# A top-k bisection step with two VectorE operations instead of three

## The chip, the cores and the metric

The kernel runs on one core of a Trainium2 chip. TensorE (PE in the profile, its weight loads PEld) multiplies matrices, VectorE (DVE) and ScalarE (ACT) work elementwise, GpSimd (POOL) does next to nothing here, and SyncE (SP) issues the DMA transfers. The metric is the device time of one execution in microseconds (us), lower being better.

## The reference

The reference is one layer of a decoder: a feed-forward half-step, a mixer of three attention branches, and a second feed-forward half-step, on 1024 rows of width 1024. What matters here is the second branch, in which each query attends to its 256 best keys. An indexer scores all earlier keys of a query; the 256th largest score of each row is the threshold.

```python
# dsa_attention, per block of 128 queries
sc = jnp.einsum('bqhd,bkd->bqhk', iqi, ik)
score = jnp.einsum('bqh,bqhk->bqk', iwi, jax.nn.relu(sc))
score = jnp.where(key_pos <= qpos, score, -jnp.inf)
_, idx = lax.top_k(score, 256)      # the selected keys
...
s = jnp.einsum('bqhd,bqkd->bqhk', qi, gather(k, idx)) * scale
p = jax.nn.softmax(jnp.where(valid, s, -jnp.inf), axis=-1)
```

The other two branches are a forgetting attention (8 heads of 64, called fox heads below) and an attention to 256 memory tokens (4 heads of 128, memory heads).

## The kernel before

Rows are handled in 8 blocks of 128. Matrices are multiplied in fp32 as high and low parts, so an operand is made by a ScalarE cast (`wH`, `th`, `ph`) and a VectorE subtraction (`wL`, `tl`, `pl`). The program runs in stages: first feed-forward half, the combined projection, the attention heads, the merge of the branches, second feed-forward half.

**The selection.** The first two blocks of rows have at most 256 keys, so only blocks 2 to 7 are selected. `select` (L937) finds the threshold of each of 128 rows by bisection over the bits of a 32-bit float. One pass is an ACTIVATE with Sign on ScalarE: it adds the candidate `nf` (tile `sn`, one number per row) to the scores `wk` (128 rows by 384 to 1024 columns), throws the result away (`junk`) and leaves the sum of the signs in `cnt` (`scnt`). From the sum VectorE makes the next candidate: `k` (`sk`) is the bit or 0, `m` (`sm`) collects the accepted bits, and `nf` is `m` with the next bit tried, flipped by `fm` (`sf`). There are 31 such steps after a first pass that finds the sign: 32 passes a block, 192 in all. A tail of about ten VectorE operations follows (`sy`, `sq`, a scan over `wk`, `mk`), which makes the mask.

**What the selection runs beside.** It is the background of two stages. In the projection stage the column blocks are mq, iq, fk, fq, fv and dq. Each chain step multiplies 24 matmuls into a bank `tm`, squares the bank on ScalarE (`hsq`), takes a sum and a reciprocal root on VectorE (`hv`, `rs_y`, `rs_a`), scales, transposes on TensorE (`turn`), and splits (`th`, `tl`). The dq blocks also rotate (`rot`), four more VectorE operations. In the attention stage first the four memory heads run, then the eight fox heads, then the eight selected heads. A head's row block is a chain: scores on TensorE (`spm` in a memory head, `sp` in the others), a row maximum on VectorE (`nmx`), the exponential on ScalarE (`ns`), transposes on TensorE (`pT`), the split `ph`, `pl`, and a product with the values (`po`). The projection of the gates (`gate`, 24 matmuls for half a tile, ended by `sg`) is filler: independent TensorE work that is put between the chains.

**What sets the order.** All engines work through their queues in order. The order is written at build time by a planner, `_Flow` (L77): it keeps a clock per engine, charges each recorded operation a cost, and lets the chain go on whose time has come. A VectorE operation on one column is charged 0.06 + 0.00105 us, after a wait of 0.13 us behind an operation of the same engine or 0.2 us behind another (L81, L91 to L96):

```python
LAT, SAME = 0.2, 0.13
wait = self.LAT if self.last != eng else 0.0 if eng == "PE" else self.SAME
start = max(self.clk[eng], self.t + wait)
```

The selection is the `background` of both runs (L1544, L1617): it is stepped whenever its time is not past the TensorE clock of the plan. `finish` (L1556) writes out whatever is left. The tile framework then places the recorded instructions in each engine's queue by its own reckoning of readiness, so the final order is read from the built program. In it, instructions that the helper classes record all have line 51.

Of the kernel before, what the change touches and what calls it, by code (L numbers as in the profile page):

```python
# [12 lines left out]
I32 = mybir.dt.int32  # L13
AF = mybir.ActivationFunctionType
OP = mybir.AluOpType
# [4 lines left out]
P = 128  # L20
# [135 lines left out]
def trunk_layer_kernel(  # L156
# [7 lines left out]
    T, A, V = fl.T, fl.A, fl.V  # L164
# [7 lines left out]
    def load(o, i):  # L172
        nc.sync.dma_start(plain(o), plain(i))

    def store(o, i):
        nc.sync.dma_start(plain(o), plain(i))
# [760 lines left out]
    def select(sp, t):  # L937
        n = (t + 1) * P
        wk = sp.tile([P, S], F32, tag="work", name="wk", bufs=3)[:, :n]
        load(wk, sc_s[t][:, :n])  # L940
        fl.t += 4.0
        yield
        junk = sp.tile([P, S], BF16, tag="junk", name="junk", bufs=1)[:, :n]
        m, k, fm, nf = [sp.tile([P, 1], I32, tag=nm, name=nm, bufs=3) for nm in ("sm", "sk", "sf", "sn")]
        cnt = sp.tile([P, 1], F32, tag="scnt", name="scnt", bufs=3)
        V.memset(m, 0)
        thr = 511.0 - n
        A.activation(junk, wk, AF.Sign, accum_out=cnt)
        V.tensor_scalar(k, cnt, thr, -1.0, op0=OP.is_ge, op1=OP.mult)
        V.tensor_scalar(fm, k, 0x7FFFFFFF, None, op0=OP.bitwise_xor)  # L950
        for b in range(30, -1, -1):
            V.scalar_tensor_tensor(nf, m, 1 << b, fm, op0=OP.bitwise_or, op1=OP.bitwise_xor)
            yield
            A.activation(junk, wk, AF.Sign, bias=nf.bitcast(F32)[:, 0:1], accum_out=cnt)
            V.tensor_scalar(k, cnt, thr, float(1 << b), op0=OP.is_ge, op1=OP.mult)
            V.tensor_tensor(m, m, k, op=OP.bitwise_or)
        V.tensor_tensor(nf, m, fm, op=OP.bitwise_xor)
        V.tensor_scalar(nf, nf, -2147483648, None, op0=OP.bitwise_xor)
        lo = nf.bitcast(F32)

        y = sp.tile([P, S], BF16, tag="sy", name="sy", bufs=1)[:, :n]
        q = sp.tile([P, S], BF16, tag="sq", name="sq", bufs=1)[:, :n]
        c2 = sp.tile([P, 4], F32, tag="sc2", name="sc2", bufs=2)
        V.tensor_scalar(y, wk, lo[:, 0:1], 0.0, op0=OP.is_gt, op1=OP.add, accum_out=c2[:, 0:1])
        yield
        V.tensor_scalar(y, wk, lo[:, 0:1], 3e38, op0=OP.is_le, op1=OP.mult)
        V.tensor_tensor_reduce(out=q, in0=y, in1=wk, scale=1.0, scalar=3e38, op0=OP.add, op1=OP.min,
                               accum_out=c2[:, 1:2])
        yield
        V.tensor_scalar(c2[:, 0:1], c2[:, 0:1], 255.5, None, op0=OP.is_gt)  # L970
        V.copy_predicated(lo, c2[:, 0:1].bitcast(I32), c2[:, 1:2])
        V.tensor_scalar(y, wk, lo[:, 0:1], 0.0, op0=OP.is_gt, op1=OP.add, accum_out=c2[:, 2:3])
        V.tensor_scalar(c2[:, 3:4], c2[:, 2:3], -1.0, 256.0, op0=OP.mult, op1=OP.add)
        yield
        V.tensor_scalar(q, wk, lo[:, 0:1], None, op0=OP.is_equal)
        yield
        one = sp.tile([P, 1], F32, tag="one", name="one", bufs=1)
        V.memset(one, 1.0)
        V.tensor_tensor_scan(wk, one.to_broadcast([P, n]), q, 0.0, OP.mult, OP.add)
        yield  # L980
        V.scalar_tensor_tensor(q, wk, c2[:, 3:4], q, op0=OP.is_le, op1=OP.mult)
        V.tensor_tensor(y, y, q, op=OP.add)
        mk = sp.tile([P, S], BF16, tag="mk", name="mk", bufs=1)[:, :n]
        V.tensor_scalar(mk, y, 1.0, BIG, op0=OP.subtract, op1=OP.mult)
        store(mask_s[t][:, :n], mk)
        yield
# [389 lines left out]
    cs, sn = tp.tile([P, NT, 32], F32, name="rope_cos"), tp.tile([P, NT, 32], F32, name="rope_sin")  # L1376
# [117 lines left out]
    def selection():  # L1494
        active, nxt = [], 2
        while active or nxt < NT:
            while len(active) < 2 and nxt < NT and nxt in sel_ready:
                active.append(chain(select(sel, nxt), start=fl.clk["PE"]))
                nxt += 1
            if not active:  # L1500
                yield fl.clk["PE"] + 5.0
                continue
            c = min(active, key=lambda c: c.t)
            fl._step(c)
            active = [c for c in active if not c.done]
            yield min([c.t for c in active], default=fl.clk["PE"])
# [111 lines left out]
    op = right["op"]  # L1618
# [97 lines left out]
```

## Time and profile before

| | |
|---|---|
| Time, median of 3 runs | 2552.32 us (2551.23 to 2557.42) |
| The profiled execution's own time | 2555.42 us |
| Its span, first to last instruction | 2553.4 us |
| Busy: TensorE / VectorE / ScalarE | 2426.6 / 1641.0 / 1146.6 us |
| First and last Sign pass of the selection | starts at 888.6 and 1368.7 us |
| Mean granted TensorE clock | 0.978 of full speed |

The profile is one execution taken by the hardware profiler. A row of its timeline gives the start in us from the beginning of the span, the duration, engine, line, operation and tiles (out<-in), and in brackets how long the engine was idle before and what ended the wait. TensorE's instructions overlap, so their pace is read from the starts.

### The profile page before, as it was taken

The page shows a single profiled execution, that of the slowest core. Times are in us where ns is not written, and L with a number is a line of the kernel's source. Part 1 is how long each engine was busy: PE and PEld are TensorE (multiplying, and loading weights), DVE is VectorE, ACT ScalarE, POOL GpSimd, SP SyncE. Part 2 cuts the span into 40 slices and gives each one's busy share as a digit, 9 for nine tenths or more (in the row PEclk, how much of TensorE's full clock was granted, in tenths as well). Part 3 has the DMA queues.
Part 4 walks back from the last instruction along what each step waited for, and adds up shares of the span by engine and source line. Part 5 has one row for each costly group of instructions (what it writes and reads, how often), then busy time and mean ns, then how long its engine had stood idle before and what let it go on. Part 6 is the DMA issues. An engine that isn't in the chain of part 4 may idle for free.

```text
span 2553.4 us, 31738 instructions
## 1 busy us (share of the span) xinstructions
PE 2426.6 (95%) x11532; PEld 2007.0 (79%) x11532; DVE 1641.0 (64%) x3405; ACT 1146.6 (45%) x1904; POOL 2.2 (0%) x40
## 2 busy tenths in 40 slices
PE   6999999999999999989999998999979999999998
PEld 4788888888777878767777886877768888888887
DVE  7855555488757578685667556777376554554885
ACT  5533333333433366657886555543144333333332
POOL 0000000000000000000000000000000000000000
PEclk9899999999999999998999999999989999999999
DMA  7222222474334534544455535756422222225743
GB/s 232 75 80 78 91 84 79 158 302 137 127 123 144 158 106 133 157 141 147 122 156 141 146 108 177 235 173 226 169 85 66 91 66 91 91 71 191 271 151 129
DMA packets 297900, 351.64 MB, mean 138 GB/s; under 512 B 18792, under 2 KB 199688, under 8 KB 297744
## 3 DMA queue, kind: packets, MB, share of 16 engines
q1 hardware_dynamic: 297744, 349.62, 42.8%
q8 instruction: 90, 1.47, 0.2%
q14 instruction: 66, 0.54, 0.1%
HBM read 254.98 MB, written 93.54 MB: 136 GB/s over the span
## 4 chain that ended last, share of the span: by engine, by line
PE 72%; DVE 12%; ACT 7%; DMA 5%; issue 4%; SPq 0%; ACTq 0%; DVEq 0%
PE gx L51 19%; PE gy L51 14%; PE tm L51 8%; PE dx L51 8%; PE dy L51 7%; PE gate L51 6%; ACT junk L51 3%; PE br L51 3%; DVE wL L51 2%; PE po L51 2%; PE pT L51 2%; PE sp L51 2%; DMA wS<-in_w_in 1%; DMA bg<-g_s 1%; ACT ns L51 1%
## 5 line engine op out<-in xcount | busy, mean ns | idle before, releaser
L51 ACT CAST wH<-wS 128x1024 fp32r<-128x1024 f32 x238 | 225.5, 953 | 303.1 <-PE gy L51 102.8
L51 PE MATMUL gx<-th,wH 128*128 128x512 f32 x880 | 318.3, 394 | 7.2 <-ACT th L51 7.2
L51 DVE TENSOR_TENSOR wL<-wS,wH 128x1024 fp32r<-128x1024 f32 x238 | 260.3, 1099 | 88.4 <-ACT wH L51 87.7
L51 PE MATMUL gx<-th,wL 128*128 128x512 f32 x704 | 275.5, 391 | 0.0
L51 PE MATMUL tm<-wH,uh 128*128 128x512 f32 x496 | 200.5, 405 | 9.2 <-ACT wH L51 5.6
L51 PE MATMUL gy<-th,wH 128*128 128x512 f32 x528 | 206.3, 391 | 1.2 <-ACT th L51 1.2
L51 PE MATMUL gx<-tl,wH 128*128 128x512 f32 x528 | 205.4, 389 | 0.0
L51 PE MATMUL gy<-th,wL 128*128 128x512 f32 x528 | 205.4, 389 | 0.0
L51 PE MATMUL gy<-tl,wH 128*128 128x512 f32 x528 | 205.4, 389 | 0.0
L51 ACT ACTIVATE junk<-wk,sn 128x384 bf16<-128x384 f32 (+5 forms) x186 | 164.3, 883 | 89.4 <-DVE sn L51 77.2
L51 PEld LDWEIGHTS gx<-th,wH 128*128 128x128 f32 x880 | 167.5, 191 | 43.1 <-ACT th L51 8.0
L51 PE MATMUL tm<-wL,uh 128*128 128x512 f32 x496 | 197.0, 397 | 1.8 <-DVE wL L51 1.0
L51 PE MATMUL tm<-wH,ul 128*128 128x512 f32 x496 | 196.6, 396 | 0.0
L51 ACT CAST wH<-S 128x1024 fp32r<-128x1024 f32 x88 | 92.3, 1051 | 170.3 <-PE gy L51 167.0
L51 DVE TENSOR_TENSOR wL<-S,wH 128x1024 fp32r<-128x1024 f32 x88 | 107.5, 1223 | 87.8 <-ACT wH L51 87.8
L51 DVE TENSOR_TENSOR gu<-gu,gy 128x512 f32<-128x512 f32 x88 | 60.3, 685 | 157.3 <-PE gy L51 81.6
L51 PE MATMUL gate<-uh,wH 128*128 128x512 f32 x384 | 157.5, 410 | 0.0
L51 DVE TENSOR_TENSOR pl<-pT,ph 128x512 fp32r<-128x512 f32 (+1 forms) x176 | 109.8, 637 | 73.6 <-ACT ph L51 72.9
L51 PEld LDWEIGHTS gx<-th,wL 128*128 128x128 f32 x704 | 133.3, 189 | 27.8
L51 PE MATMUL gate<-uh,wL 128*128 128x512 f32 x384 | 153.4, 400 | 0.0
L51 PE MATMUL gate<-ul,wH 128*128 128x512 f32 x384 | 153.0, 398 | 0.0
L51 PE MATMUL dx<-wH 128*128 128x512 f32 x352 | 137.5, 391 | 2.2 <-DVE rows L51 2.1
(265 smaller groups left out, 5196.9 us busy)
## 6 DMA issues: line engine op xcount, KB each, us to landing
wS<-in_ffn_w_down SPq DMA_DIRECT2D x70, 512.0 KB
wS<-in_w_in SPq DMA_DIRECT2D x48, 512.0 KB
wS<-in_ffn_w_gate SPq DMA_DIRECT2D x44, 512.0 KB
wS<-in_ffn_w_up SPq DMA_DIRECT2D x44, 512.0 KB
hid_s<-gu SPq DMA_DIRECT2D x44, 512.0 KB
a<-hid_s SPq DMA_DIRECT2D x30, 512.0 KB
g_s<-sg SPq DMA_DIRECT2D x48, 256.0 KB
bg<-g_s SPq DMA_DIRECT2D x48, 256.0 KB
```

Source lines behind the costliest of these rows:

```text
L51: return fn(*a, **k)
```

## The change

The tiles `m` and `fm` are dropped. `nf` itself is carried from step to step: it starts as the first candidate; after a pass `k` is the bit if it is *not* accepted (`is_lt` instead of `is_ge`), and one operation flips that bit back and the next bit over. After the last bit the sign bit is flipped in the same way, so the two operations behind the loop go too, and the memset ahead of it. A step has two VectorE operations instead of three, `select` 64 instead of 98; over six blocks that is 204 fewer. The Sign passes and the tail are as before.

```diff
-        m, k, fm, nf = [sp.tile([P, 1], I32, tag=nm, name=nm, bufs=3) for nm in ("sm", "sk", "sf", "sn")]
+        k, nf = [sp.tile([P, 1], I32, tag=nm, name=nm, bufs=3) for nm in ("sk", "sn")]
         cnt = sp.tile([P, 1], F32, tag="scnt", name="scnt", bufs=3)
-        V.memset(m, 0)
         thr = 511.0 - n
+
         A.activation(junk, wk, AF.Sign, accum_out=cnt)
         V.tensor_scalar(k, cnt, thr, -1.0, op0=OP.is_ge, op1=OP.mult)
-        V.tensor_scalar(fm, k, 0x7FFFFFFF, None, op0=OP.bitwise_xor)
+        V.tensor_scalar(nf, k, 0x3FFFFFFF, None, op0=OP.bitwise_xor)
         for b in range(30, -1, -1):
-            V.scalar_tensor_tensor(nf, m, 1 << b, fm, op0=OP.bitwise_or, op1=OP.bitwise_xor)
             yield
             A.activation(junk, wk, AF.Sign, bias=nf.bitcast(F32)[:, 0:1], accum_out=cnt)
-            V.tensor_scalar(k, cnt, thr, float(1 << b), op0=OP.is_ge, op1=OP.mult)
-            V.tensor_tensor(m, m, k, op=OP.bitwise_or)
-        V.tensor_tensor(nf, m, fm, op=OP.bitwise_xor)
-        V.tensor_scalar(nf, nf, -2147483648, None, op0=OP.bitwise_xor)
+            V.tensor_scalar(k, cnt, thr, float(1 << b), op0=OP.is_lt, op1=OP.mult)
+            V.scalar_tensor_tensor(nf, k, (1 << b - 1) if b else -2147483648, nf, op0=OP.bitwise_or, op1=OP.bitwise_xor)
         lo = nf.bitcast(F32)
```

Because the planner charges every recorded operation, the dropped ones move everything that it places after them. From the first selection on, the queues of TensorE, VectorE, ScalarE and SyncE stand in another order, up to the second feed-forward half.

TensorE's queue in the memory heads, before, where the third memory head begins (the number of a tile tells heads apart; `spm_9533` are the scores, `pT_9550` the transposes of their exponential):

```order
L51 MATMUL rT_9519<-ident_69,sums_8945 8x128
L51 MATMUL spm_9533<-km_9489,qs_9487 128x256 x2
L51 MATMUL spm_9533<-km_9489,vs_9488 128x256
L51 MATMUL spm_9533<-km_9489,qs_9487 128x256 x2
L51 MATMUL spm_9533<-km_9489,vs_9488 128x256
L51 MATMUL pT_9550<-ident_69,ns_9540 128x128
L51 MATMUL spm_9563<-km_9526,qs_9524 128x256 x2
L51 MATMUL spm_9563<-km_9526,vs_9525 128x256
```

And now, at the same place (the scores are `spm_9413`, the transposes `pT_9445`):

```order
L51 MATMUL spm_9413<-km_9371,qs_9369 128x256 x2
L51 MATMUL spm_9413<-km_9371,vs_9370 128x256
L51 MATMUL gate_9429<-uh_4806,wH_9211 128x512
L51 MATMUL gate_9429<-ul_4807,wH_9211 128x512
L51 MATMUL gate_9429<-uh_4806,wL_9212 128x512
...
L51 MATMUL pT_9445<-ident_69,ns_9420 128x128
```

Before, the first transpose stands directly behind the scores whose exponential it needs; now 12 gate matmuls (three shown, the other nine repeat them) stand between.

ScalarE's queue in the dq blocks of the projection, before (`hsq` squares a block's bank, `th` casts its transpose, `junk` are the passes of the fourth selected block of rows, 768 columns):

```order
L51 CAST th_8641<-turn_8636 128x512
L51 ACTIVATE hsq_8606<-tm_8581 128x512
L51 ACTIVATE junk_9216,scnt_9221<-wk_9151,sn_9220 128x768
L51 CAST th_8699<-turn_8694 128x512
L51 ACTIVATE hsq_8672<-tm_8647 128x512
L51 ACTIVATE junk_9216,scnt_9221<-wk_9151,sn_9220 128x768
L51 ACTIVATE hsq_8730<-tm_8705 128x512
```

And now:

```order
L51 ACTIVATE hsq_8475<-tm_8450 128x512
L51 CAST th_8502<-turn_8497 128x512
L51 ACTIVATE junk_9079,scnt_9082<-wk_9030,sn_9081 128x768 x3
L51 ACTIVATE hsq_8533<-tm_8508 128x512
L51 CAST th_8566<-turn_8561 128x512
L51 ACTIVATE junk_9079,scnt_9082<-wk_9030,sn_9081 128x768 x3
L51 ACTIVATE hsq_8597<-tm_8572 128x512
```

Where one pass stood between two squares, three stand there now, for six blocks in a row. In the whole queue 112 of the 192 passes stood ahead of the first exponential of a memory head; now 130 do.

SyncE's queue where the first memory head's operands are loaded, before (`dq_s` is the last store of the projection, `wS` the weights of a later gate, `qs`, `vs`, `km` the head's operands):

```order
L176 DMA dq_s_87<-th_8890 128x4x128
L176 DMA dq_s_87<-tl_8891 128x4x128
L173 DMA wS_9373<-in_w_in 128x8x128
L173 DMA qs_8928<-mq_s_91 128x1024
L173 DMA vs_8929<-mq_s_91 128x1024
L173 DMA km_8930<-km_s_92 128x512
```

And now:

```order
L176 DMA dq_s_87<-th_8790 128x4x128
L176 DMA dq_s_87<-tl_8791 128x4x128
L173 DMA qs_8831<-mq_s_91 128x1024
L173 DMA vs_8832<-mq_s_91 128x1024
L173 DMA km_8833<-km_s_92 128x512
```

The weight load has gone from ahead of the head's operands to behind them.

VectorE's queue at the tail of the first selected block of rows, before (`sy`, `sq` belong to the tail, `rs_a`, `rs_y` to the block whose transposes TensorE is to do next, `wL` to weights, `sm`, `sk`, `sf`, `sn` to the next selection):

```order
L51 TENSOR_SCALAR sy_8761<-wk_6673,sn_6711 128x384
L51 TENSOR_TENSOR rs_a_7342<-rs_a_7342,hv_7338 128x8
L51 TENSOR_TENSOR wL_7401<-wS_7398,wH_7400 128x1024
L51 TENSOR_SCALAR sk_6823<-scnt_6826 128x1
L51 SCALAR_TENSOR_TENSOR rs_a_7342<-rs_a_7342 128x8
L51 ISA sq_8762,sc2_8763<-sy_8761,wk_6673 128x384
L51 ISA sc2_8763 128x1
L51 TENSOR_TENSOR sm_6822<-sm_6822,sk_6823 128x1
L51 SCALAR_TENSOR_TENSOR rs_y_7341<-rs_a_7342,rs_y_7341 128x8
L51 TENSOR_TENSOR wL_7413<-wS_7410,wH_7412 128x1024
```

And now:

```order
L51 TENSOR_SCALAR sy_8680<-wk_6673,sn_6709 128x384
L51 TENSOR_SCALAR sn_6797<-sk_6796 128x1
L51 TENSOR_SCALAR sc2_8682<-sc2_8682 128x1
L51 ISA sq_8681,sc2_8682<-sy_8680,wk_6673 128x384
L51 ISA sc2_8682 128x1
L51 COPY_PREDICATED sn_6709<-sc2_8682 128x1
L51 TENSOR_SCALAR sy_8680,sc2_8682<-wk_6673,sn_6709 128x384
```

Before, the tail stood amid one block's root and two weight splits; now it stands together, with neither between its operations, and the next block's sum (`hv`) comes behind it.

## Rows read from the trace of the kernel before

**Rows 1.** Busy time of each engine in three stretches: the projection beside the selection, the memory heads, and the first fox heads up to the end of the selection. Columns: the stretch, its length, busy us (and instructions) of PE, PEld, DVE, ACT and POOL, the granted TensorE clock, the DMA share and GB/s.
```profile
888.00:1139.00 251.00, 238.75 (x1078) 193.37 (x1078) 199.56 (x754) 156.34 (x322) 0.00 (x0) 0.98 0.43 127
1139.00:1260.00 121.00, 102.94 (x546) 85.57 (x544) 64.75 (x253) 95.00 (x224) 0.00 (x0) 0.90 0.52 168
1260.00:1390.00 130.00, 124.34 (x718) 102.03 (x718) 96.99 (x303) 101.61 (x201) 0.00 (x0) 1.00 0.51 141
```
**Rows 2.** TensorE's waits from 888 to 1139 us: who waited for whom, us in total, times, longest.
```profile
PE turn L51 <- DVE hv L51: 3.3, 1, 3.3
PE tm L51 <- DVE hsq L51: 3.1, 1, 3.1
PE tm L51 <- ACT wH L51: 2.1, 1, 2.1
```
**Rows 3.** The same from 1139 to 1390 us.
```profile
PE pT L51 <- ACT ns L51: 10.5, 10, 3.7
PE spm L51 <- DMA km<-km_s: 6.8, 2, 4.6
PE po L51 <- DVE pl L51: 3.5, 6, 1.4
```
**Rows 4.** One step of the bisection at 768 columns, with what SyncE issued just before, from the timeline of all engines.
```profile
1137.74 0.55 SPq L173 DMA_DIRECT2D wS<-in_w_in  x1
...
1138.07 0.94 ACT L51 ACTIVATE junk<-wk,sn 128x768 bf16<-128x768 f32 x1 [0.67 <-DVE sn L51]
...
1138.91 0.19 ACT L51 ACTIVATION_READ_ACCUMULATOR junk<-wk,sn 128x1 f32 x1
1139.13 0.15 DVE L51 TENSOR_SCALAR sk<-scnt 128x1 int32<-128x1 f32 x1 [1.16 <-ACT junk L51]
...
1139.32 0.16 DVE L51 TENSOR_TENSOR sm<-sm,sk 128x1 int32<-128x1 int32 x1
1139.52 0.16 DVE L51 SCALAR_TENSOR_TENSOR sn<-sm,sf 128x1 int32<-128x1 int32 x1
...
1139.77 0.94 ACT L51 ACTIVATE junk<-wk,sn 128x768 bf16<-128x768 f32 x1 [0.67 <-DVE sn L51]
```
**Rows 5.** The group of one dropped operation between 888 and 1390 us: busy us, mean ns, idle time before.
```profile
L51 DVE TENSOR_TENSOR sm<-sm,sk 128x1 int32<-128x1 int32 x186 | 29.2, 157 | 4.3
```
**Rows 6.** VectorE's timeline while the first selected block ends and the queue is full.
```profile
950.38 0.14 DVE L51 TENSOR_SCALAR sn<-sn 128x1 int32<-128x1 int32 x1
950.44 0.14 DVE L51 TENSOR_SCALAR sk<-scnt 128x1 int32<-128x1 f32 x1
950.50 0.17 DVE L51 TENSOR_SCALAR hv<-hv 128x8 f32<-128x8 f32 x1
...
954.29 1.22 DVE L51 TENSOR_TENSOR wL<-wS,wH 128x1024 fp32r<-128x1024 f32 x1
```
**Rows 7.** TensorE's timeline at its waits.
```profile
957.39 0.75 PE L51 MATMUL turn<-ident,hsq 128*128 128x128 f32 x4 [3.30 <-DVE hv L51]
...
1107.86 0.67 PE L51 MATMUL tm<-wH,uh 128*128 128x512 f32 x1 [3.11 <-DVE hsq L51]
...
1196.45 0.39 PE L51 MATMUL gate<-ul,wH 128*128 128x512 f32 x1
1196.68 0.39 PE L51 MATMUL gate<-uh,wL 128*128 128x512 f32 x1
...
1201.55 0.47 PE L51 MATMUL pT<-ident,ns 128*128 128x128 f32 x1 [3.66 <-ACT ns L51]
...
1245.05 0.44 PE L51 MATMUL po<-ph,vs 128*128 128x256 f32 x2 [0.87 <-ACT ph L51]
...
1249.98 0.51 PE L51 MATMUL po<-ph,vs 128*128 128x256 f32 x2 [0.94 <-ACT ph L51]
...
1253.50 0.48 PE L51 MATMUL pT<-ident,ns 128*128 128x128 f32 x1 [1.81 <-ACT ns L51]
```
**Rows 8.** Busy time and granted clock right after three of these waits (columns as in Rows 1).
```profile
1107.90:1109.00 1.10, 1.10 (x3) 0.91 (x4) 1.10 (x3) 0.00 (x0) 0.00 (x0) 0.53 0.44 131
1201.60:1204.60 3.00, 3.00 (x13) 2.81 (x14) 0.64 (x3) 1.96 (x5) 0.00 (x0) 0.50 0.46 145
1253.50:1255.80 2.30, 2.30 (x7) 1.90 (x8) 0.61 (x4) 1.97 (x6) 0.00 (x0) 0.50 0.00 0
```
**Rows 9.** ScalarE's timeline in the dq blocks.
```profile
1122.24 0.60 ACT L51 ACTIVATE hsq<-tm 128x512 f32<-128x512 f32 x1 [2.27 <-PE turn L51]
1122.73 0.58 ACT L51 CAST th<-turn 128x512 fp32r<-128x512 f32 x1
1123.19 0.95 ACT L51 ACTIVATE junk<-wk,sn 128x768 bf16<-128x768 f32 x1
...
1128.15 0.60 ACT L51 ACTIVATE hsq<-tm 128x512 f32<-128x512 f32 x1 [2.22 <-PE turn L51]
...
1130.30 0.94 ACT L51 ACTIVATE junk<-wk,sn 128x768 bf16<-128x768 f32 x1 [0.57 <-DVE sn L51]
...
1132.64 0.94 ACT L51 ACTIVATE junk<-wk,sn 128x768 bf16<-128x768 f32 x1 [0.24 <-DVE sn L51]
```
**Rows 10.** VectorE's timeline in the dq blocks.
```profile
1121.56 0.75 DVE L51 TENSOR_TENSOR rot<-hsq,sgq 128x256 f32<-128x256 f32 x2
1122.23 0.15 DVE L51 SCALAR_TENSOR_TENSOR sn<-sm,sf 128x1 int32<-128x1 int32 x1
1122.34 0.69 DVE L51 TENSOR_TENSOR hsq<-hsq,rot 128x512 f32<-128x512 f32 x1
```

## The prediction

> **What bounds the kernel now.** I first read the busy time by stretch, since the change touches only what lies beside the selection. TensorE bounds all of it. From 888 to 1139 us it is busy for 238.75 of 251 us; in the memory heads, 1139 to 1260 us, for 102.94 of 121 us, at a granted clock of 0.90; in the first fox heads, to 1390 us, for 124.34 of 130 us [rows 1]. So at most 12.25 + 18.06 + 5.66 = 36 us of idle time is there to win, plus what a low clock costs: (1 - 0.98) x 251 = 5 us and (1 - 0.90) x 121 = 12 us at most, since part of the low clock falls on idle time. VectorE (361 of 502 us busy in these stretches) is not the bound, and shortening its work counts only where TensorE waits for it, or for ScalarE behind it.
>
> Next come TensorE's waits. In the projection there are three large ones: 3.3 us for the sum `hv`, 3.1 for `hsq`, 2.1 for a weight cast [rows 2]. In the heads, transposes waited 10.5 us for exponentials, the first memory head 6.8 us for its operands from memory, products 3.5 us for `pl` [rows 3]. The operations of the bisection release little themselves; they are what stands ahead in the queues.
>
> Last, one step. A pass starts at 1138.07; its sum is read at 1138.91; `sk`, `sm`, `sn` start at 1139.13, 1139.32, 1139.52; the next pass starts at 1139.77 [rows 4]. The step takes 1.70 us, and 0.20 of it is the operation that goes (start to start). ScalarE sits idle for 0.67 us in each such step, with whatever stands behind the pass.
>
> **The change part by part.** It removes 204 VectorE operations; of the 186 of one kind each has 157 ns and together they were busy for 29.2 us [rows 5]. The merged operation has the form of the old `sn` (one column, int32, two bitwise operations), 0.16 us [rows 4]; I take that, and nothing in the rows puts it further than 0.03 us off.
>
> What VectorE gains by it depends on the queue. On a chain the operation costs 0.20 us. In a full queue independent small operations start 0.06 us apart although each lasts 0.14 [rows 6]. So the 204 give back between 204 x 0.06 = 12 us and 204 x 0.20 = 41 us of VectorE's time, none of it TensorE's. The Trainium skill, "Perfetto Trace Analysis", section "Optimizing Scalar/DVE Operations", says that a profiled duration is about twice the time that the engine is held, because the second half overlaps with the next instruction. The rows agree (0.14 against 0.06), and by that rule the busy time of 29 us counts as 15 rather than 29 us; neither is a term below, where TensorE's waits are counted instead.
>
> Off TensorE's path, then, the direct gain is zero, and what matters is what the new order does to the waits. By the order, passes go faster against TensorE's work: 130 instead of 112 lie before the memory heads. I go through the places.
>
> Third memory head. TensorE waited 3.66 us at 1201.55, because a transpose stood directly behind its scores [rows 7], and then ran 3.0 us at clock 0.50, which costs 1.5 us [rows 8]: 5.2 us. Now 12 gate matmuls stand between, at 0.23 us from start to start [rows 7], 2.8 us. That leaves 0.9 us of wait; the low clock of Rows 8 came behind waits of 3 us or several in a row, so I let it go too: -4.3 us. At worst the exponential comes later behind the denser passes, and nothing is won; at best 5.2.
>
> From the memory heads to the fox heads. Waits of 0.87, 0.94 and 1.81 us [rows 7], then 2.3 us at clock 0.50 [rows 8], 1.15 lost: 4.8 us. Counted in the order, four score blocks there had their transposes behind them at less than 0.7 us of TensorE work (matmuls between them by 0.23 us); now two have. Half of it: -2.4 us (0 to -4.8).
>
> First memory head. The load of weights that SyncE issued for 0.55 us ahead of the head's operands [rows 4] now stands behind them. TensorE's wait of 4.6 us for `km` [rows 3] falls by that much at least, if nothing else holds the loads; by more if the transfers shared the memory. I take -1 us (0 to -3).
>
> Tails of the selections. At 957.39 TensorE had waited 3.30 us [rows 7] while the tail, a root and two weight splits of 1.22 us [rows 6] took turns on VectorE. The tail now stands in one piece without the splits. Half: -1.7 us (+2 to -3.3). At 1107.86 it had waited 3.11 us [rows 7], with 1.1 us at clock 0.53 after it [rows 8], together 3.6 us, for the same reason with the third tail, which fell into the dq blocks. In the new order the third tail comes in the fv blocks, which have no root, and the fourth where TensorE waits for `km` anyway: -3.6 us (0 to -3.6).
>
> Dq blocks. Here the change can cost. Three passes instead of one or two stand between two squares in ScalarE's queue, six blocks in a row. A TensorE-paced block takes 5.91 us (`hsq` to `hsq`, 1122.24 to 1128.15) [rows 9]. Three passes of 1.50 us (1.70 - 0.20) are 4.5; square and cast take 0.49 + 0.46 [rows 9]; and in the new order `sn` stands twice behind a VectorE operation of this block, about 0.65 us (0.67 for `rot`, some 0.6 for `hsq` [rows 10]): 4.5 + 0.95 + 1.3 = 6.75 us, 0.84 over the block's pace. Six times that is +5 us. The lower bound is 0 (banks of `tm` in reserve swallow it); the upper comes from two passes that stood 2.34 us apart there (1130.30, 1132.64) [rows 9]: 3 x 2.34 + 0.95 = 7.97, 2.06 over, +12.4 us, plus up to 0.5 us of low clock per block as after 1107.86: +15.
>
> Sum: -4.3 - 2.4 - 1.0 - 1.7 - 3.6 + 5.0 = -8.0 us. The profiled execution took 2555.42 us, so it would take 2547.4; it was 3.1 us above the median of 2552.32. On the median I forecast 2544.3, say **2544 us**. The weight wait of 2.1 us [rows 2] I leave as it is. The later heads are reshuffled too, but the order there has as many tight places as before; that is a spread of some 5 us either way, not a term.
>
> **The rivals.**
>
> *Slower: the dq blocks become a closed loop of ScalarE and VectorE.* A square waits behind three passes, each pass behind `sn`, `sn` behind the block's own VectorE work, which waits for the square. At the upper price, +15 us, with the memory-head waits re-formed elsewhere (0 instead of -6.7) and -1 - 1.7 - 3.6 kept, it ends at +8.7: 2561 us. Without the dq blocks my sum is -13.0, so it decides at 13.0 / 6 = 2.2 us a block. For it: two passes did stand 2.34 us apart there, though only one was in a block's way [rows 9]. Against it: in those steps ScalarE also waited for TensorE (2.27 and 2.22 us before the squares [rows 9]), time that a denser queue can use.
>
> *No change: stalls move.* TensorE bounds, and a plan of the same kind puts new tight places where the old were. The waits of the two memory-head places come back elsewhere (+6.7) and the others stand: -1.3 in sum, 2551 us. The rule in the Trainium skill, "Perfetto Trace Analysis", section "Identifying the Most-Contended Engine", speaks for this: work on the engine with the highest occupancy first, and that is not VectorE. Here TensorE's busy share bears it out, but the waits for VectorE and ScalarE do not [rows 2, 3].
>
> *More: ScalarE is freed for the heads.* Each pass blocks ScalarE's queue 0.20 us less, and 18 fewer passes are left for the heads. If the heads' waits apart from `km` go, 18.06 - 6.8 = 11.3 us in the memory heads, with 1.5 + 1.15 of clock, and 3.3 + 3.1 + 0.5 in the projection, and the dq blocks cost nothing: -20.9 - 1 = -22: 2530 us. Against it: the passes stay as dense per us of TensorE's work until they are used up.
>
> *The step does not get shorter.* Were the merged operation as long as the two, only the order would change; the rows of `sn` (0.16 us) give no reason, and I give it no chance of its own.
>
> **How the numbers follow.** The forecast with its own range of 2536 to 2552 has 0.44, no change 0.22, more 0.18, slower 0.16. A measurement here can tell 0.3%, 7.7 us, from no change: below 2544.7 is faster, above 2560.0 slower. The forecast lies on that edge, so it gives 0.27 to faster and 0.17 to the same; no change gives 0.18 to the same, 0.02 to faster, 0.02 to slower; more is faster, 0.18; slower gives 0.12 to slower, 0.04 to the same. Together faster 0.47, same 0.39, slower 0.14. The range reaches to both outer cases: 2528 to 2561.
>
> **What would show it.** Right: `sk` to `sn` to the next pass with 0.45 instead of 0.64 us from the start of `sk`; the wait at the third memory head under 1.5 us and no low clock there; no wait of 3 us behind a VectorE tail in the projection; the last pass some 20 to 40 us earlier than 1368.7. Wrong: dq blocks more than 6.9 us from square to square; waits for exponentials from 1139 to 1390 us as large as the 10.5 us of Rows 3; or a gain that lies after 1390 us, which would be the reshuffling and not this argument.

## The result, and the profile after

The changed kernel takes 2540.60 us (median of 6 runs, 2535.67 to 2544.91), the kernel before 2553.28 us beside it (2551.23 to 2559.48): a ratio of 0.9945, 95% interval 0.9933 to 0.9958. Timed again later (in the last series below) it took 2543.45 us beside 2551.58, a ratio of 0.9962 (0.9949 to 0.9976). So the change is worth some 8 to 14 us, by these medians and ratios. The forecast was 2544 us, and faster as the likeliest verdict. The time came out right, but the argument behind it was half wrong, and the experiments show which half.

The profiled execution of the changed kernel took 2544.91 us, the longest of the six; its span is 2542.9 us. Busy are TensorE 2419.0, VectorE 1617.0 and ScalarE 1147.4 us; VectorE lost 24 us. First, the same three stretches as in [rows 1], with the same columns:

```profile
888.00:1139.00 251.00, 236.47 (x1074) 190.26 (x1073) 197.37 (x700) 181.25 (x368) 0.00 (x0) 0.99 0.45 136
1139.00:1260.00 121.00, 105.13 (x574) 87.63 (x573) 63.98 (x207) 97.30 (x223) 0.00 (x0) 0.92 0.49 158
1260.00:1390.00 130.00, 126.69 (x742) 105.01 (x742) 80.65 (x213) 82.56 (x166) 0.00 (x0) 1.00 0.52 143
```

ScalarE did 25 us more in the projection and 19 us less in the fox heads: the passes moved forward. The last one starts at 1299.8 instead of 1368.7 us. TensorE is hardly busier in the memory heads (105.13 against 102.94) and slightly less so in the projection. One step of the bisection, to set beside [rows 4]:

```profile
1131.83 0.15 DVE L51 TENSOR_SCALAR sk<-scnt 128x1 int32<-128x1 f32 x1 [0.34 <-ACT junk L51]
...
1132.02 0.16 DVE L51 SCALAR_TENSOR_TENSOR sn<-sk,sn 128x1 int32<-128x1 int32 x1
...
1132.27 0.94 ACT L51 ACTIVATE junk<-wk,sn 128x768 bf16<-128x768 f32 x1 [0.48 <-DVE sn L51]
...
1133.78 0.94 ACT L51 ACTIVATE junk<-wk,sn 128x768 bf16<-128x768 f32 x1 [0.47 <-DVE sn L51]
```

From `sk` to the next pass it is 0.44 us (0.64 before), from pass to pass 1.51 (1.70). The step became 0.19 us shorter, as the prediction had it. TensorE's waits, from 888 to 1139 us and from 1139 to 1390 us, answering to [rows 2] and [rows 3] (us in total, times, longest):

```profile
PE turn L51 <- DVE hsq L51: 3.7, 2, 3.2
PE spm L51 <- DMA km<-km_s: 3.5, 1, 3.5
PE isc L51 <- DVE sk L51: 1.9, 2, 1.6
...
PE pT L51 <- ACT ns L51: 8.1, 5, 3.9
PE sp L51 <- DMA ks<-fk_s: 3.8, 1, 3.8
PE spm L51 <- DMA km<-km_s: 3.2, 1, 3.2
PE po L51 <- DVE pl L51: 2.3, 2, 1.2
```

The 3.3 us for `hv`, the 3.1 for `hsq` and the 2.1 for a weight cast are gone; other waits of the same size have come. Where they stand is told by TensorE's timeline, for [rows 7]:

```profile
1012.84 0.63 PE L51 MATMUL turn<-ident,hsq 128*128 128x128 f32 x4 [3.18 <-DVE hsq L51]
...
1194.25 0.39 PE L51 MATMUL gate<-uh,wL 128*128 128x512 f32 x1
1194.61 0.33 PE L51 MATMUL pT<-ident,ns 128*128 128x128 f32 x1
...
1236.59 0.77 PE L51 MATMUL sp<-ks,qs 128*128 128x128 f32 x2 [3.85 <-DMA ks<-fk_s]
...
1244.68 0.47 PE L51 MATMUL pT<-ident,ns 128*128 128x128 f32 x1 [3.94 <-ACT ns L51]
```

At 1194.61 us the third memory head's transposes follow the gates without a bracket: no wait. The passage to the fox heads, at 1236 and 1244 us, got worse. And the dq blocks, for [rows 9]:

```profile
1098.30 0.60 ACT L51 ACTIVATE hsq<-tm 128x512 f32<-128x512 f32 x1 [0.30 <-DVE sk L51]
...
1100.78 0.94 ACT L51 ACTIVATE junk<-wk,sn 128x768 bf16<-128x768 f32 x1 [0.48 <-DVE rs_a L51]
...
1102.86 0.94 ACT L51 ACTIVATE junk<-wk,sn 128x768 bf16<-128x768 f32 x1 [1.05 <-DVE sn L51]
...
1104.19 0.60 ACT L51 ACTIVATE hsq<-tm 128x512 f32<-128x512 f32 x1 [0.30 <-DVE sk L51]
```

Three passes stand in a block, and still it takes 5.89 us from square to square, against 5.91 before.

### The profile page after: what moved, and what is told of

Same layout as the page of the kernel before. It is cut to its first block, busy times and chain, and to the rows that moved or that the text cites. A ratio compares the mean times of both kernels' runs of the same rounds, so it can differ in the third digit from the quotient of the medians.

```text
span 2542.9 us, 31538 instructions
## 1 busy us (share of the span) xinstructions
PE 2419.0 (95%) x11532; PEld 2001.3 (79%) x11532; DVE 1617.0 (64%) x3201; ACT 1147.4 (45%) x1904; POOL 2.2 (0%) x40
## 4 chain that ended last, share of the span: by engine, by line
PE 79%; DVE 9%; ACT 6%; DMA 3%; issue 3%; SPq 0%; ACTq 0%; DVEq 0%
PE gx L51 19%; PE gy L51 14%; PE tm L51 9%; PE gate L51 8%; PE dx L51 8%; PE dy L51 7%; PE br L51 4%; ACT junk L51 3%; PE po L51 2%; PE pT L51 2%; PE sp L51 2%; DVE wL L51 2%; PE nar L51 1%; PE isc L51 1%; DMA wS<-in_w_in 1%
## 5 line engine op out<-in xcount | busy, mean ns | idle before, releaser
L51 ACT ACTIVATE junk<-wk,sn 128x384 bf16<-128x384 f32 (+5 forms) x186 | 164.2, 883 | 64.6 <-DVE sn L51 55.4
```

The source lines that it names most:

```text
L51: return fn(*a, **k)
```

## The experiments

The changed kernel differs from the one before in two ways at once: its operations are fewer, and all queues stand in another order. My theory at this point was that the second made the gain. The first four kernels take the two apart.

**Operations and order, crossed.** Two kernels have every engine's queue held in a given order. The planner is charged as in the kernel that gives the order; each recorded instruction is noted and, before the framework arranges the queues, chained as a stored table says (an edge that orders only and makes nothing wait):

```diff
+    for n, runs in json.loads(zlib.decompress(base64.b64decode(QUEUES))).items():
+        row = [_seen[n][i] for p, m in runs for i in range(p, p + m)]
+        for a, b in zip(row, row[1:]):
+            tc.add_manual_dep(b, a.name, mybir.DependencyInfo(
+                mybir.DependencyClass.NoSync, mybir.DependencyReason.DATA), reason="hold")
```

In the built programs the instructions of TensorE, ScalarE, GpSimd and SyncE then stand exactly as in the kernel that gave the order, and so they ran in the traces; VectorE differs by the operations of the step alone. The other two change only what the planner is charged:

```diff
 # new operations, old costs
+        fl.charge("DVE", 0.06055)
...
+            fl.charge("DVE", 0.06105)
             yield
 # old operations, new costs
-        V.memset(m, 0)
+        nc.vector.memset(m, 0)
...
-            V.scalar_tensor_tensor(nf, m, 1 << b, fm, op0=OP.bitwise_or, op1=OP.bitwise_xor)
+            nc.vector.scalar_tensor_tensor(nf, m, 1 << b, fm, op0=OP.bitwise_or, op1=OP.bitwise_xor)
```

Expected of the new operations in the old order:

> The two-operation step with every engine's queue held in the order of the kernel before (same rows on TensorE, ScalarE and SyncE; VectorE's queue only without the dropped operations). Theory (most of the gain comes from the queues being laid out anew once the planner believes the steps to be shorter): 2548 to 2553 us, at most 4 us of the 12.7 us gained. Rival 1 (the 0.2 us saved in a step does it by itself, wherever the queues stand): 2540 to 2543 us. Rival 2 (the new order is luck and the operations are nothing): 2552 to 2555 us, the same as before.

Expected of the old operations in the new order:

> The three-operation step with every engine's queue held in the order of the changed kernel (same rows on TensorE, ScalarE and SyncE; VectorE's queue with the two old operations put back behind their predecessor). Theory: 2543 to 2547 us, that is the old operations give back under half of the 12.7 us. Rival 1 (the shorter step by itself): 2551 to 2555 us. Rival 2 (order is all): 2540 to 2542 us, the same as the changed kernel.

Expected of the two with exchanged costs:

> The two-operation step, but the planner is still charged for the dropped operations, so that it emits exactly the order it emitted before; the framework's own scheduler then arranges the queues from it with the shorter step. Theory: between the first run of this series and the changed kernel, 2543 to 2551 us. Rival 1 (shorter step by itself): 2540 to 2543 us. Rival 2 (order is luck): anywhere from 2540 to 2560 us, without relation to the number of operations.

> The three-operation step, but the planner is charged only for two operations, so that it emits the order of the changed kernel; the framework's scheduler then arranges the queues with the longer step. Theory: a plan that thinks the selection shorter than it is leaves passes late, 2545 to 2552 us. Rival 1 (shorter step by itself): 2551 to 2556 us. Rival 2 (order is luck): anywhere from 2540 to 2560 us.

Measured (before beside them: 2553.18 us):

| queues | three operations | two operations |
|---|---|---|
| order of before, held | 2553.18 (the kernel before) | 2538.76, ratio 0.9935 (0.9922 to 0.9947) |
| order of the changed kernel, held | 2567.20, ratio 1.0046 (1.0033 to 1.0059) | 2540.60 (the changed kernel, above) |
| planner charged for three | 2553.18 (the kernel before) | 2548.85, ratio 0.9977 (0.9966 to 0.9987) |
| planner charged for two | 2550.55, ratio 0.9986 (0.9975 to 0.9997) | 2540.60 (the changed kernel) |

My theory fell. With no row of TensorE or ScalarE moved, the shorter step alone gains 14 us; in the new order it is worth 27. The new order by itself gains nothing: with the old operations it costs 14 us, with the new ones it is even. Luck of the order is real and of the same size: the same two operations took 2538.8, 2540.6 and 2548.9 us in three arrangements, the same three operations 2550.6, 2553.2 and 2567.2. Where only the planner's costs are held, the step is worth 4 us (charged for three) and 10 us (charged for two). In all four comparisons the shorter step is ahead, but the slowest arrangement with two operations can't be told from the fastest with three (0.9977 and 0.9986, the intervals overlap).

Since the first of these kernels has TensorE's queue word for word as before, the same matmul can be looked up in both traces. Here are rows of both, first of the kernel before (three more stand in [rows 7]) and then with the short step:

```profile
889.64 0.74 PE L51 MATMUL isc<-ikk,iqs 128*128 128x512 f32 x2 [0.38 <-DVE sk L51]
...
1074.85 0.50 PE L51 MATMUL tm<-wH,uh 128*128 128x512 f32 x1 [2.10 <-ACT wH L51]
...
1384.05 0.50 PE L51 MATMUL po<-pl,vs 128*128 128x256 f32 x2 [0.97 <-DVE pl L51]
```

```profile
890.98 0.73 PE L189 MATMUL isc<-ikk,iqs 128*128 128x512 f32 x2 [0.78 <-DVE sk L189]
...
956.75 0.63 PE L189 MATMUL turn<-ident,hsq 128*128 128x128 f32 x4 [2.25 <-DVE hv L189]
...
1100.34 0.47 PE L189 MATMUL tm<-wH,uh 128*128 128x512 f32 x1 [2.35 <-DVE hsq L189]
...
1190.86 0.33 PE L189 MATMUL pT<-ident,ns 128*128 128x128 f32 x1 [2.31 <-ACT ns L189]
...
1367.94 0.50 PE L189 MATMUL po<-pl,vs 128*128 128x256 f32 x2 [0.94 <-DVE pl L189]
```

At 889.64 the short step is 1.34 us late, at 1384.05 it is 16.11 us ahead: 17.45 us were won in between. The waits of [rows 7] shrink where they stood: 3.30 to 2.25, 3.11 to 2.35, 3.66 to 2.31 us. The one of 2.10 us at 1074.85, which the prediction left as it was, is gone. Between the same two matmuls, before and then with the short step (columns as in [rows 1]):

```profile
889.64:1384.05 494.41, 459.14 (x2296) 375.36 (x2296) 353.70 (x1290) 348.29 (x731) 0.00 (x0) 0.97 0.48 141
890.98:1367.94 476.96, 451.16 (x2296) 371.25 (x2296) 331.74 (x1089) 348.01 (x731) 0.00 (x0) 0.98 0.49 146
```

TensorE's idle time there, length less busy time, fell from 35.3 to 25.8 us, 9.5 less. Its busy time for the same 2296 matmuls fell by the other 8.0 us. Most of that is the clock: the traces have 34.1 us at half speed in this stretch before and 20.5 us here, which is worth 6.8 us at most. (This execution took 2532.36 us, the shortest of its six; the 7 us that it is ahead beyond 1384 us come in code that is the same, and the kernel before itself spreads from 2547.83 to 2558.17.)

What took the wait at 1074.85 away is seen on ScalarE, before and with the short step:

```profile
1072.94 0.83 ACT L51 ACTIVATE junk<-wk,sn 128x640 bf16<-128x640 f32 x1 [0.67 <-DVE sn L51]
...
1073.77 1.03 ACT L51 CAST wH<-wS 128x1024 fp32r<-128x1024 f32 x1
```

```profile
1066.70 0.83 ACT L189 ACTIVATE junk<-wk,sn 128x640 bf16<-128x640 f32 x1 [0.48 <-DVE sn L189]
...
1067.63 1.05 ACT L189 CAST wH<-wS 128x1024 fp32r<-128x1024 f32 x1
```

The cast of the next weights stands behind a pass, and the pass behind a candidate that VectorE has still to make. The pass ran 6.24 us earlier, though TensorE came only 3.44 us earlier to the matmul that waited for the cast. That is the mechanism as these rows show it: ScalarE stood idle at the head of its queue 0.67 us in each such step, 0.48 now, and what stood behind, the casts, squares and exponentials that TensorE needs, had to wait that long. It is not the whole. Of TensorE's waits in the stretch, those that ended with ScalarE fell from 14.8 to 9.4 us, but those that ended with VectorE also fell, from some 13 to some 9. Whether it was room on VectorE that did this is tested next.

**Chain or room on VectorE, and where.** The next four test that. All hold the order of before. One puts a third operation back that nothing waits for; one has a single operation (the threshold writes the next candidate itself and the merge is left out, so this kernel does not compute the selection); two use the short step in three of the six selections:

```diff
 # idle operation beside the chain
             V.scalar_tensor_tensor(nf, k, ..., nf, op0=OP.bitwise_or, op1=OP.bitwise_xor)
+            _note("DVE", nc.vector.tensor_tensor(xx, k, k, op=OP.bitwise_or))
 # one operation
-            V.tensor_scalar(k, cnt, thr, float(1 << b), op0=OP.is_lt, op1=OP.mult)
-            V.scalar_tensor_tensor(nf, k, ..., nf, op0=OP.bitwise_or, op1=OP.bitwise_xor)
+            V.tensor_scalar(nf, cnt, thr, float(1 << b), op0=OP.is_lt, op1=OP.mult)
 # half of the selections
+        new = t < 5        # the other kernel: t >= 5
```

> The two-operation step in the held order of the kernel before, with a third one-column operation put back behind it on VectorE that nothing waits for (so VectorE's queue has its old number of operations, but the chain from sum to next pass stays short). Theory, as the first four runs leave it (the chain is what counts: each pass ends 0.2 us sooner and with it all that stands behind it on ScalarE): 2538 to 2543 us. Rival (room on VectorE's queue is what counts): 2549 to 2554 us.

> A step with one VectorE operation, in the held order of the kernel before: the threshold operation writes the next bias itself and the merging operation is left out, so the bisection's result is not computed. Theory (the chain of pass and operations): another 0.2 us a step; the largest tight places are gone already, so less than the first 14 us: 2528 to 2535 us. Rival 1 (what could be won is won, TensorE bounds): 2537 to 2540 us. Rival 2 (proportional to the step's length): 2523 to 2526 us.

> Held order of the kernel before; the two-operation step only in the first three selections (384, 512 and 640 columns, whose passes lie under the projection), the old step in the last three. Theory (the gain is local to where the passes run: about 7 us of it came between 890 and 1135 us in the trace of the first run): 2544 to 2549 us. Rival (the memory heads give it all): 2551 to 2554 us.

> Held order of the kernel before; the two-operation step only in the last three selections (768, 896 and 1024 columns, whose passes reach from 1100 us through the memory heads to the fox heads), the old step in the first three. Theory: the other half, 2543 to 2549 us, and both halves add up to the whole within 3 us. Rival (the memory heads give it all): 2538 to 2541 us.

Measured, with before at 2553.27 us: 2536.49 us with the idle operation (ratio 0.9942, 0.9929 to 0.9954), 2531.63 with one operation (0.9915, 0.9902 to 0.9928), 2545.20 with the first three selections short (0.9969, 0.9954 to 0.9984), 2545.73 with the last three (0.9971, 0.9961 to 0.9981).

All four came out as the theory of the chain had them (the first 1.5 us below its range). An operation on VectorE beside the chain costs nothing that can be measured, though it stands in the same queue:

```profile
1141.08 0.15 DVE L189 TENSOR_SCALAR sk<-scnt 128x1 int32<-128x1 f32 x1
1141.26 0.16 DVE L189 SCALAR_TENSOR_TENSOR sn<-sk,sn 128x1 int32<-128x1 int32 x1
1141.34 0.15 DVE L1098 TENSOR_TENSOR sx<-sk 128x1 int32<-128x1 int32 x1
1141.52 0.94 ACT L189 ACTIVATE junk<-wk,sn 128x768 bf16<-128x768 f32 x1 [0.68 <-DVE sx L1098]
```

`sx` starts 0.08 us behind `sn`, and the pass 0.26 us behind `sn`, as without it (0.25). The bracket names `sx`, the last that ended before the pass; but the pass reads `sn` and not `sx`. So a releaser in this view is a guess where two end close together. ScalarE's idle time ahead of its passes is 58.1 us in this trace, against 57.2 without the idle operation, and the waits that VectorE ended at 957.39 and 1107.86 (times of before) are 2.32 and 2.55 us, against 2.25 and 2.35: the 186 operations put back on VectorE did not lengthen them again. Between the same two matmuls as above this trace gained 13.0 us, not 17.45; two executions with the same short step differ by that much. By length of the chain ScalarE's waits ahead of its passes fall in step: the group of the passes, with three, two and one operation in one and the same order (busy, mean ns, idle before):

```profile
L51 ACT ACTIVATE junk<-wk,sn 128x384 bf16<-128x384 f32 (+5 forms) x186 | 164.3, 883 | 89.4 <-DVE sn L51 77.2 <-DVE rs_a L51 5.8 <-DVE one L51 3.0
```

```profile
L189 ACT ACTIVATE junk<-wk,sn 128x384 bf16<-128x384 f32 (+5 forms) x186 | 164.4, 884 | 57.2 <-DVE sn L189 53.9 <-DVE rs_y L189 1.6 <-DVE rs_a L189 1.4
```

```profile
L185 ACT ACTIVATE junk<-wk,sn 128x384 bf16<-128x384 f32 (+5 forms) x186 | 164.3, 883 | 33.7 <-DVE sn L185 33.6
```

89.4, 57.2 and 33.7 us, and 2553, 2539 and 2532 us of time: 32 us less idle gave 14 us, a further 24 gave 7. In the new order the same group has 94.5 us with three operations and 64.6 with two, for 2567 and 2541 us. The chain holds up VectorE too, at `sk`, which waits for the sum of the pass: VectorE's idle time ahead of `sk` is 95.5, 89.2 and 80.1 us with three, two and one operation. So the length of the chain is shown as the cause; how much of the gain went through ScalarE's queue and how much through VectorE's is not told apart. The two halves of the selection gave 8.1 and 7.5 us, together 15.6, about the whole 14.4. And each half acts where its passes run. The third memory head's wait with the first three selections short, and then with the last three:

```profile
1192.62 0.48 PE L190 MATMUL pT<-ident,ns 128*128 128x128 f32 x1 [3.66 <-ACT ns L190]
```

```profile
1201.85 0.33 PE L191 MATMUL pT<-ident,ns 128*128 128x128 f32 x1 [2.30 <-ACT ns L191]
```

3.66 us as before with the first, 2.30 with the second. Against the kernel before, the first kernel is 8.70 us ahead at 1107.86 and 8.34 at 1384.05, so nothing more is won in the heads; the second is 3.57 us late at 1145.88 and 4.89 ahead at 1384.05.

**What the new order gives back.** The waits of 3.85 and 3.94 us at the passage to the fox heads are ScalarE's and SyncE's order. Three kernels hold the order of the changed kernel and move rows there:

```diff
 # SyncE (the loads alone in one kernel)
-r_s<-rs, qs, o_s<-os, r_s<-rs, qs, ks x4, vs
+qs, qs, ks x4, r_s<-rs, vs, o_s<-os, r_s<-rs
 # ScalarE (VectorE alike: ns<-sp,cb x4 ahead of sk, sn of four steps)
-junk x4, ns x4
+ns x4, junk x4
 # the last kernel: ScalarE
-ns x4, junk x4, ph, junk x2, ph, ...
+ns x4, ph, junk, ph, ...      (five passes go to 1299 to 1312 us)
```

> The changed kernel in its own order, with three rows moved at the passage from the memory heads to the fox heads: the second fox head's loads of ks ahead of three small stores on SyncE, its four masked copies ahead of four bisection steps on VectorE, its four exponentials ahead of the same four passes on ScalarE. Theory (there the new order lost what the shorter step had won: waits of 3.85 and 3.94 us and a stretch of low clock of 13.7 us in the trace of the changed kernel): both waits under 1.5 us, the low clock shorter, 2530 to 2535 us. Rival 1 (the passes put off make the same wait a little later): 2538 to 2542 us. Rival 2 (only one of the waits goes, the clock stays low): 2535 to 2538 us.

> The same with SyncE's rows moved alone. Theory: the wait for ks falls from 3.85 to about 1 us, but the exponential stands behind the passes as before and so the next wait grows by what the first one lost: 2538 to 2541 us. Rival (the loads were the cause of both waits): 2532 to 2536 us.

> The changed kernel itself beside the two, on the same chip, as their base: 2538 to 2543 us by every theory.

Measured (before 2551.58 us): 2543.69 us mended (ratio 0.9961, 0.9946 to 0.9976), 2541.69 with the loads alone (0.9956, 0.9942 to 0.9970), 2543.45 unmended (0.9962, 0.9949 to 0.9976). The 2530 to 2535 us expected of the mended kernel were missed: against the unmended one nothing is gained. Mended, TensorE's waits at this place and what ScalarE did ahead of the last of them:

```profile
1234.21 0.47 PE L188 MATMUL sp<-ks,qs 128*128 128x128 f32 x2 [1.87 <-DMA ks<-fk_s]
...
1237.96 0.33 PE L188 MATMUL pT<-ident,ns 128*128 128x128 f32 x1 [0.62 <-ACT ns L188]
...
1246.40 0.45 PE L188 MATMUL po<-ph,vs 128*128 128x256 f32 x2 [4.67 <-ACT ph L188]
```

```profile
1244.74 1.15 ACT L188 ACTIVATE junk<-wk,sn 128x1024 bf16<-128x1024 f32 x1 [0.47 <-DVE sn L188]
1245.89 0.46 ACT L188 CAST ph<-pT 128x384 fp32r<-128x384 f32 x1
```

Both waits fell, 3.85 to 1.87 and 3.94 to 0.62, and a new one of 4.67 us came: the four passes, put behind the exponentials, now stood ahead of the cast of `ph`. That is what the first rival said. The Trainium skill, "PSUM — Partial Sum Buffer", section "Engine vs sequencer instructions", calls ScalarE's queue strictly first in, first out; the rows agree, the cast waits behind four passes that it has nothing to do with. With the loads alone the wait for `ks` fell to 2.74 us, not to about 1, and the next grew to 6.46 us, by more than the first had lost. The last kernel puts the passes elsewhere:

> The mended kernel of the ninth run once more, with the passes of the last selection put where ScalarE has room: of the six passes that stood between 1239 and 1250 us in its trace, behind which a cast of ph kept TensorE waiting for 4.67 us, one stays behind that cast and five go to the end of the chain (1299 to 1312 us), with their VectorE operations, the rest of that selection 12 us later. The selection's last result is read by the score masks only from 1483 us on. Theory (it was the place of the passes, and there is a place where they cost nothing): no wait over 1.5 us between 1236 and 1260 us, about 5 us less than the ninth run: 2536 to 2540 us. Rival (ScalarE is short of time in the whole passage, so the wait moves on again): 2541 to 2545 us.

```profile
1235.52 0.47 PE L188 MATMUL sp<-ks,qs 128*128 128x128 f32 x2 [3.36 <-DMA ks<-fk_s]
...
1239.06 0.48 PE L188 MATMUL pT<-ident,ns 128*128 128x128 f32 x1 [0.36 <-ACT ns L188]
...
1300.77 0.45 PE L188 MATMUL po<-ph,vs 128*128 128x256 f32 x2 [1.60 <-ACT ph L188]
```

2538.66 us (2534.95 to 2545.74), ratio 0.9947 (0.9930 to 0.9964). The wait for `ph` is gone from this place and ScalarE no longer stops TensorE there; that for `ks` is 3.36 us, over the 1.5 expected, and where the passes went there are new ones of 1.60, 0.91 and 1.21 us. Matmul by matmul against the trace of the unmended kernel, 4.2 us are won between 1236 and 1260 us and 5.0 lost between 1290 and 1400: in this execution, its slowest, the wait moved on, as the rival had it. The median is in the expected range, but the interval overlaps with that of the unmended kernel, so a gain is not shown. No kernel was found that beats the changed one beyond doubt; the nearest that compute everything are the short step in the old order, 0.9935, and the same with the idle operation, 0.9942.

## Why the prediction was right and wrong

The step itself came as predicted: 0.19 us shorter, `sk` to pass 0.44 us.

The step of the argument that failed is the sentence "Off TensorE's path, then, the direct gain is zero, and what matters is what the new order does to the waits." The direct gain is all there is: 14.4 us with no row moved. I had noted that ScalarE sits idle in each step "with whatever stands behind the pass", and did not follow it to the casts and exponentials behind. What the new order does to the waits came to nothing with the short step and to a loss of 14 us with the long one. The time was right by luck: the two errors made about the same sum, because waits that I let go for the order's sake shrank for the chain's.

The mechanism stood among the rivals. "Each pass blocks ScalarE's queue 0.20 us less" is what the runs bear out, but that rival had a chance of 0.18 and a price of 22 us, since it let nearly every wait in the heads go. With the order held, waits for exponentials fell only from 10.5 to 7.6 us between the two matmuls above, and the two for `km` stayed (6.8 and 6.7).

Term by term:
- *Third memory head* (-4.3 us): won; there is no wait and no low clock. But the gates between, to which the term was ascribed, are only part of the cause. In the old order, with no gate between, 3.66 us fell to 2.31 and the clock right after the wait (0.50 in [rows 8]) stayed at 1.00; the same matmuls gained 3.8 us across this place.
- *Third tail* (-3.6): gone as said. *First tail* (-1.7): the wait for `hv` at 957 went, but a wait of 3.18 us stands at the second tail (1012.84), so nothing is left of this term. The sign "no wait of 3 us behind a VectorE tail in the projection" did not come.
- *Dq blocks* (+5, the only cost): mis-sized, it is 0. I let `sn` stand twice behind an operation of the block; it does so once (the wait of 1.05 us at 1102.86), the other pass waits 0.48. No wait of TensorE lies between these squares: 5.89 us a block is its own pace. The upper price of this term also counted a cast twice: between the two passes 2.34 us apart ScalarE ran a `th`, at 1131.82 us.
- *Passage to the fox heads* (-2.4): wrong sign. Two waits of 3.85 and 3.94 us stand there with a low clock, where 0.87, 0.94 and 1.81 stood. I had counted score blocks with too little cover behind them; what decided were six passes of 1024 columns in a row ahead of the exponentials, and loads behind stores.
- *First memory head* (-1): `km` is waited for 3.5 + 3.2 us, 6.8 before: nothing.
- *The last pass* comes 69 us earlier, not 20 to 40. No price of it is seen: the masks are read only from 1483 us on (in the trace of the mended kernel).
- *Stretch of the gain*: between 888 and 1390 us, as said. By the number of matmuls done, the changed kernel is 2.7 us late at 896 us and 6.4 ahead at 1393, 9.1 us of the 10.5 between the two spans.

The slower rival's mechanism exists, though not with this step. With the three operations in the same order, ScalarE's squares stand 6.27 us apart:

```profile
1122.11 0.58 ACT L189 ACTIVATE hsq<-tm 128x512 f32<-128x512 f32 x1
...
1128.38 0.58 ACT L189 ACTIVATE hsq<-tm 128x512 f32<-128x512 f32 x1
```

That is 0.38 us a block over TensorE's pace, and a wait of 3.35 us for a turn follows at 1142.50 in that trace. The rival needed the operation that the change takes away.

The rival of no change had beside it the advice of the Trainium skill, "Perfetto Trace Analysis", section "Identifying the Most-Contended Engine", to optimize the engine with the highest occupancy first. Here TensorE was that engine (95% of the span), and its idle time and low clock were shortened on a chain between two others. The Trainium skill, "Perfetto Trace Analysis", section "Optimizing Scalar/DVE Operations", says that larger operations help if the engine is saturated, and for engines that are not, but cause bubbles elsewhere, it names splitting work. VectorE was busy for 64% of the span; one operation fewer on the chain helped all the same, and one more beside it did no harm.

What stays open: why the short step is worth 27 us in the new order and 14 in the old. Matmul by matmul the traces put 24.7 us of it where the selection runs (880 to 1390 us), 16.1 of them idle time of TensorE, and show more of the same: 8.6 us between 1121 and 1157 us of the changed kernel, where with three operations a transpose had waited 5.00 us for an exponential and a turn 3.35. No kernel was made that takes them apart.

## What to carry to other kernels

Price a dependent chain between two engines by what stands behind it in the queues of the engines that wait, not by whether its own operations are on the critical path: here a pass that waited held up the casts and exponentials behind it. Where an edit also moves the order, hold the order of both kernels by explicit edges and cross the two; arrangements of the same operations lay 10 and 17 us apart here, and the cross tells that from the edit. A single wait mended by hand came back a little later each time it was tried here; ask first where the queue has room.

## What was not expected of the hardware

The third VectorE operation of a step cost 0.19 us when the next depended on it and nothing measurable when nothing did (2536.49 against 2538.76 us), in the same place of the same queue. And up to 6.8 of the 17.45 us won in the old order were TensorE's clock. At the third memory head the granted share was 0.50 for 3 us after a wait of 3.66 us [rows 8], and 1.00 after the 2.31 us that remained of it. The length of the wait alone does not decide that: after the 2.25 us at 956.75 in the same trace it was 0.50. Both stretches with the short step, in order of time:

```profile
957.80:960.80 3.00, 3.00 (x9) 2.33 (x8) 2.74 (x8) 2.74 (x6) 0.00 (x0) 0.50 0.58 162
1190.90:1193.90 3.00, 3.00 (x18) 2.69 (x19) 1.49 (x5) 1.96 (x6) 0.00 (x0) 1.00 0.50 156
```
